# The mLSTM's output gate as a fifth seven-product pair

## The chip, the cores and the metric

The kernel runs on one core of one Trainium2 chip. The metric is the device time of one execution in microseconds (us), as the median of several runs. A profile is one execution taken by the hardware profiler. The engines are TensorE (PE in the profile, its weight loads PEld), VectorE (DVE), ScalarE (ACT), GpSimd (POOL) and SyncE (SP, which issues most of the DMA transfers).

## The reference

One layer of an encoder for 256 tokens of width 2048, all in float32: a SwiGLU feed-forward block, a mixer, a second feed-forward block, each followed by a layer norm, and an input embedding at the end. The mixer, which is all that the change touches, projects its input once and runs two branches:

```python
proj = x @ w_in                                   # 2048 -> 11272 columns
mq, mk, mv, mo, mi, mf, sq, sk, sv, ga, gb = _split_cols(proj)
qk = jax.nn.silu(_causal_conv(jnp.concatenate([mq, mk], axis=-1), conv_w))
...
h = _mlstm_chunkwise(q heads, k heads, v heads, log_i, log_f)       # 4 heads of 256
h = _head_norm(h, norm_g)
y_m = h * jax.nn.sigmoid(mo)                                        # mo: 1024 columns, the output gate
y_sb = _stick_breaking(_heads(sq, 8), _heads(sk, 8), _heads(sv, 8)) # 8 heads of 128
merged = jax.nn.sigmoid(ga) * (y_m @ w_up_m) + jax.nn.sigmoid(gb) * (y_sb @ w_up_sb)
return merged @ w_out
```

## The kernel before, in words

**Matmuls.** The activations stand transposed in on-chip memory as two parts, a rounded high part and the remainder; every weight tile is split in the same way. A product takes three matmuls (high x high, high x low, low x high: lines 1213 to 1215). The work is cut in *units*: one weight tile of 256 rows by up to 512 columns, one half (128) of the 256 tokens, six matmuls. An ordinary column group of 512 needs 8 weight tiles x 2 token halves = 16 units, and each weight tile serves two units.

**Seven products.** `seven` (line 321) computes two column groups at once, as a 2 x 2 block product with seven instead of eight block products: 28 units instead of 32. Some of its products need sums of weight tiles: `grow` (line 337) adds a second tile during a DMA that the GpSimd queue issues, `plus` (line 342) adds on VectorE. Each of its units has a weight tile of its own to split. Its intermediate results go through two reserved accumulator banks (`seeded`). The merge gates ga and gb (four pairs, `gates7`) and most of the feed-forward blocks already use it.

**Weights on their way.** A raw tile is loaded by SyncE (line 1135), rounded by ScalarE (line 1162), and VectorE subtracts to get the low part (line 1166). Raw tiles, split tiles and most other data share 44 buffers of one size, called pages. How many raw tiles and split tiles the plan holds at a time is set by `rooms`: in the mixer 8 to 13 raw tiles and, over the woven part, 4 split tiles; the feed-forward blocks use 16 and 5.

**Order.** The kernel is unrolled by a planner in Python. The list `main` holds the ordinary units: the columns of q, k, v, the output gate and the attention branch, then part of the up projection. `chained` makes a list of the four pairs with gaps between their products, and `weave` spreads this side list evenly over `main`. After each unit the planner's clock advances and generators that are due emit their steps, with the waits in `DELAY` (us) between steps: the convolution (`conv`), the mLSTM heads (`mlstm`), the attention heads (`stick`). Every engine carries out its instructions in the order in which the planner emitted them. `wait` holds a generator until flags are set; it is a wait of the planner, not of an engine.

**The output gate.** `main` has 16 units for each of two column groups g; `mo_done` applies the sigmoid straight from the accumulator and lets GpSimd multiply by the head norm's weights (line 790). Heads 2g and 2g+1 are spawned just ahead of these units, begin when their q, k, v and the gates i and f are there, and wait for the output gate late, ahead of line 857, where the normalised head is multiplied by it. In a head, line 817 is the first matmul, line 821 a select on GpSimd, lines 828 and 840 the further matmuls, line 866 the transposes. In `stick`, lines 882 and 895 to 896 are the first matmuls, 891 and 900 selects on GpSimd, and line 906 the last matmuls, which read what line 900 writes; `DELAY["s2"]` stands between them. Line 677 transposes columns of the attention branch for `sb_turn`, and line 683 copies them out. `away` and `back` put the finished mLSTM output into device memory and fetch it again (line 808). `sched.until` steps generators ahead of their due time when a buffer is lacking.

Of the kernel before, what the change touches and what calls it, by code (L numbers as in the profile page):

```python
# [10 lines left out]
ACT = mybir.ActivationFunctionType  # L11
ALU = mybir.AluOpType
# [4 lines left out]
D = 2048  # L17
# [6 lines left out]
COL = 512  # L24
# [19 lines left out]
DELAY = {  # L44
    "gb": 12.0, "form": 14.0, "form1": 30.0, "ln_turn": 3.4, "ln_step": 1.2, "ln_low": 2.6, "h": 8.0, "silu": 6.0, "late": 9.0, "rest": 1.2, "mt": 3.2,
    "sbt": 6.0, "g0": 3.0, "g1": 4.0, "g2": 12.0, "cv0": 1.0, "cv1": 6.0, "turn": 3.5, "apart": 9.0, "copied": 2.5, "away": 6.0, "refill": 14.0, "cv2": 1.3,
    "m0": 3.0, "m1": 0.6, "m2": 1.2, "m3": 4.6, "m4": 4.6, "s0": 6.6, "s1": 6.7, "s2": 4.0,
}


# [106 lines left out]
def weave(main, side):  # L157

    n = sum(isinstance(u, Unit) for u in main)
    out, at, seen = [], 0, 0  # L160
    for u in main:
        out.append(u)
        if isinstance(u, Unit):
            seen += 1
            while at < len(side) and at * n < seen * len(side):
                if side[at] is not None:
                    out.append(side[at])
                at += 1
    return out
# [11 lines left out]
def kernel(  # L181
# [23 lines left out]
    sched = Sched()  # L205
# [13 lines left out]
    def big(shape=(P, 1024)):  # L219
        return page_pool.tile(list(shape), F32, name="big", tag="page")  # L220
# [16 lines left out]
    def activate(out, in_, func, **kw):  # L237
        use_table(func)
        nc.scalar.activation(out, in_, func, **kw)  # L239
# [11 lines left out]
    xres = [res_pool.tile([P, D], F32, name=f"xres{t}") for t in range(TT)]  # L251
# [136 lines left out]
    program = []  # L388

    def rooms(*n):  # L390
        return lambda: room.__setitem__(slice(0, len(n)), n)
# [5 lines left out]
    class Norm:  # L397
# [206 lines left out]
    st = {}  # L604
# [43 lines left out]
    def wait(*names):  # L648
        while not all(f in flags for f in names):
            yield 0.6  # L650
# [84 lines left out]
    def qk_done(which, g):  # L735
        stage = {}

        def done(ps, t):
            stage[t] = temp()
            nc.scalar.copy(stage[t][:], ps)  # L740
            if t == TT - 1:
                sched.spawn(conv(which, g, stage), DELAY["cv0"])
        return done
# [37 lines left out]
        st["nm"] = big()  # L781
        nc.sync.dma_start(out=st["nm"][:], in_=norm_m[0].partition_broadcast(P))

    def mo_done(g):
        def done(ps, t):
            if ("mo", t) not in st:
                st["mo", t] = big()
            cs = slice(g * COL, (g + 1) * COL)
            activate(st["mo", t][:, cs], ps, ACT.Sigmoid)
            nc.gpsimd.tensor_tensor(out=st["mo", t][:, cs], in0=st["mo", t][:, cs],  # L790
                                    in1=st["nm"][:, cs], op=ALU.mult)
            flags.add(("mo", t, g))
# [18 lines left out]
        return tl[:, 0:512].rearrange("q (a s) -> q a s", s=S)[:, :, 0:P]  # L811

    def mlstm(h):
        yield from wait("gates", ("qk", 0, h), ("qk", 1, h), ("v", 0, h // 2), ("v", 1, h // 2))
        d = temp()
        ps = misc([P, S])
        nc.tensor.matmul(ps[:], st["sel"][:, h], st["M"], start=True, stop=True)
# [39 lines left out]
        nc.vector.reciprocal(out=rstd[:], in_=rstd[:])  # L857
        for t in range(TT):
            nc.vector.tensor_scalar(out=hs[:, t], in0=hs[:, t], scalar1=mv[:, t, 0:1], scalar2=rstd[:, t],
# [85 lines left out]
    ga0 = sq0 + 3 * HS * DS  # L945
    gt = {}

    def gates7(g):

        def place(t, half):  # L950
            if (g, t) not in gt:
                assert g > 1 or "spilt" in flags
                gt[g, t] = xres[t][:, g * 1024:(g + 1) * 1024] if g < 2 else big()[:]
            return gt[g, t][:, half * COL:(half + 1) * COL]

        def done(m, banks):
            ps = {k: v["ps"][:] for k, v in banks.items() if v}
            if m == 5:
                e = temp()
                nc.scalar.copy(e[:], ps["E"])  # L960
                banks["B"]["ps"], banks["W"]["ps"] = seeded
                nc.vector.tensor_tensor(out=banks["B"]["ps"][:], in0=ps["X"], in1=e[:], op=ALU.subtract)
                drop()
            elif m == 6:
                nc.scalar.copy(banks["W"]["ps"][:], ps["B"])
            elif m == 4:
                nc.scalar.copy(place(1, 0), ps["E"])
            elif m == 2:
                sched.spawn(gate(0, 0, ps["X"], 1.0), DELAY["silu"])
            elif m == 7:  # L970
                c = place(1, 0)
                nc.vector.tensor_tensor(out=c, in0=ps["W"], in1=c, op=ALU.add)
                sched.spawn(gate(1, 0, c, 1.0), DELAY["silu"])
            elif m == 3:
                sched.spawn(gate(0, 1, ps["B"], -1.0))
                sched.spawn(gate(1, 1, ps["W"], -1.0))
# [7 lines left out]
        return seven(w_in[:, ga0:ga0 + D], w_in[:, ga0 + D:ga0 + 2 * D], D, g * COL, COL, x1T, done)  # L984

    def up_done(g, half):
        def done(ps, t):
# [19 lines left out]
    main.insert(len(main) - 4, back)  # L1007
# [245 lines left out]
```

## Time and profile before

| | |
|---|---|
| median of 3 runs | 2197.73 us (2196.45 to 2198.91) |
| the profiled execution | 2197.17 us, of which the span from first to last instruction is 2195.5 us |
| TensorE busy | 2175.7 us (99%) |
| VectorE busy | 1789.3 us (82%) |
| ScalarE busy | 1333.5 us (61%) |
| GpSimd busy | 241.2 us (11%) |

Busy times say how long an engine had something in work. TensorE's matmuls overlap one another, so its speed is read from the spacing of its matmuls. In groups of instructions, "x8 | 10.0, 1245 | 29.2" is the count, the busy time in us, the mean of one in ns, and the engine's idle time before them, with what ended it. In lists of waits a row names who waited, on what, and the total in us, the number of times and the longest. "L1166" is line 1166 of the kernel.

### The profile page before, as it was taken

Reading aid. Unit: us, or ns where it says so; the run is one execution under the profiler, and the core shown is the slowest. Engines: PE = TensorE matmul, PEld = TensorE weight load, DVE = VectorE, ACT = ScalarE, POOL = GpSimd, SP = SyncE. Lnnn points to the kernel's source line nnn. Section 1 sums busy time; section 2 is a strip of 40 time slices with the busy share of each in tenths; the row PEclk is TensorE's granted clock in tenths of the full one; section 3 lists DMA queues with packets and bytes.
Section 4 is the critical chain, followed back from the end, with each engine's and each line's share of the span. In section 5 each row is a group of like instructions: output and inputs, shape, how many; then the busy total and the mean of one; then the engine's idle time right before and its main releaser. Section 6 shows DMA issues by size and latency. Waiting matters only on the chain.

```text
span 2195.5 us, 27768 instructions
## 1 busy us (share of the span) xinstructions
PE 2175.7 (99%) x9972; PEld 1801.3 (82%) x9972; DVE 1789.3 (82%) x1967; ACT 1333.5 (61%) x1600; POOL 241.2 (11%) x209
## 2 busy tenths in 40 slices
PE   9999999999999999999999999999999999999999
PEld 7888888888887888888887888888888888888878
DVE  6889988888898778877676777599898989889884
ACT  6556565666575666766575644556666666666562
POOL 3111101111100001011022100011011101110000
PEclk9999999999999999999999999999999999999999
DMA  9899889887993858879678876679878998899652
GB/s 347 221 256 268 254 240 301 270 245 208 292 328 115 255 140 255 225 225 270 206 196 252 261 265 200 213 161 316 262 228 243 305 259 248 241 278 300 214 167 72
DMA packets 274346, 527.06 MB, mean 240 GB/s; under 512 B 16640, under 2 KB 25760, under 8 KB 273952
## 3 DMA queue, kind: packets, MB, share of 16 engines
q1 hardware_dynamic: 229248, 435.10, 58.5%
q0 software_dynamic: 44960, 90.19, 22.4%
q8 instruction: 78, 1.28, 0.2%
q14 instruction: 60, 0.49, 0.1%
HBM read 518.93 MB, written 6.29 MB: 239 GB/s over the span
## 4 chain that ended last, share of the span: by engine, by line
PE 94%; DVE 2%; ACT 2%; issue 1%; DMA 1%; POOL 0%; DVEq 0%; ACTq 0%
PE mm L1214 26%; PE mm L1215 25%; PE mm L1213 25%; PE seeded L1214 5%; PE seeded L1215 5%; PE seeded L1213 5%; PE ms L267 1%; DVE split L1166 1%; ACT split L1162 1%; DMA aside<-actT 1%; ACT temp L239 0%; PE ms L456 0%; POOL temp L891 0%; PE ms L906 0%; PE ms L840 0%
## 5 line engine op out<-in xcount | busy, mean ns | idle before, releaser
L1166 DVE TENSOR_TENSOR split<-raw,split 128x1024 fp32r<-128x1024 f32 (+2 forms) x1061 | 1241.6, 1205 | 221.5 <-ACT split L1162 209.5
L1162 ACT CAST split<-raw 128x1024 fp32r<-128x1024 f32 (+2 forms) x1061 | 1066.8, 1038 | 443.0 <-PE mm L1214 119.1
L1213 PE MATMUL mm<-split,actT 128*128 128x512 f32 (+2 forms) x2640 | 1026.7, 389 | 2.8 <-ACT big L1069 2.3
L1214 PE MATMUL mm<-split,actT 128*128 128x512 f32 (+2 forms) x2640 | 1015.3, 385 | 4.7 <-DVE split L1166 4.7
L1215 PE MATMUL mm<-split,actT 128*128 128x512 f32 (+2 forms) x2640 | 1015.3, 385 | 2.3 <-DVE actT L272 2.3
L1214 PEld LDWEIGHTS mm<-split,actT 128*128 128x128 f32 x2640 | 496.4, 188 | 103.0 <-DVE split L1166 8.3
L1215 PEld LDWEIGHTS mm<-split,actT 128*128 128x128 f32 x2640 | 495.9, 188 | 102.1 <-DVE actT L272 3.1
L1213 PEld LDWEIGHTS mm<-split,actT 128*128 128x128 f32 x2640 | 496.2, 188 | 99.7 <-ACT big L1069 3.2
L337 POOL DMA_DIRECT2D raw<-in_ffn_w_dram x128 | 153.9, 1216 | 1159.8 <-DVE split L1166 961.9
L342 DVE TENSOR_TENSOR raw<-raw 128x1024 f32<-128x1024 f32 x160 | 195.3, 1221 | 12.8 <-DMA raw<-in_ffn_w_dram 10.6
L1214 PE MATMUL seeded<-split,actT 128*128 128x512 f32 x480 | 187.1, 390 | 1.8 <-DVE split L1166 1.8
L1213 PE MATMUL seeded<-split,actT 128*128 128x512 f32 x480 | 188.6, 393 | 0.0
L1215 PE MATMUL seeded<-split,actT 128*128 128x512 f32 x480 | 187.0, 390 | 0.0
L571 DVE SCALAR_TENSOR_TENSOR xres<-mm,xres 128x512 f32<-128x512 f32 x160 | 109.1, 686 | 21.9 <-PE mm L1215 21.9
L1214 PEld LDWEIGHTS seeded<-split,actT 128*128 128x128 f32 x480 | 90.2, 188 | 20.6 <-DVE split L1166 2.5
L1215 PEld LDWEIGHTS seeded<-split,actT 128*128 128x128 f32 x480 | 90.1, 188 | 18.8
L1213 PEld LDWEIGHTS seeded<-split,actT 128*128 128x128 f32 x480 | 90.2, 188 | 18.0
L269 ACT CAST actT<-ms 128x512 fp32r<-128x512 f32 x60 | 35.2, 587 | 85.2 <-PE ms L267 85.1
L337 POOL DMA_DIRECT2D raw<-in_w_in_dram x32 | 38.5, 1208 | 269.8 <-DVE split L1166 262.8
L272 DVE TENSOR_TENSOR actT<-ms,actT 128x512 fp32r<-128x512 f32 x60 | 41.1, 686 | 25.0 <-ACT actT L269 15.2
L239 ACT ACTIVATE temp<-mm 128x512 f32<-128x512 f32 (+1 forms) x38 | 21.8, 574 | 57.8 <-PE mm L1215 57.8
L235 ACT ACT_TABLE_LOAD x36 | 46.2, 1283 | 0.6
(154 smaller groups left out, 724.5 us busy)
## 6 DMA issues: line engine op xcount, KB each, us to landing
raw<-in_ffn_w_dram SPq DMA_DIRECT2D x527, 512.0 KB, 8.0
raw<-in_w_in_dram SPq DMA_DIRECT2D x168, 512.0 KB, 5.0
raw<-in_ffn_w_dram POOLq DMA_DIRECT2D x128, 512.0 KB, 9.4
raw<-in_w_in_dram POOLq DMA_DIRECT2D x32, 512.0 KB, 8.1
raw<-in_w_out_dram SPq DMA_DIRECT2D x32, 512.0 KB, 4.9
raw<-in_w_ple_gate_dram SPq DMA_DIRECT2D x24, 512.0 KB, 5.4
raw<-in_w_up_m_dram SPq DMA_DIRECT2D x16, 512.0 KB, 5.3
raw<-in_w_up_sb_dram SPq DMA_DIRECT2D x16, 512.0 KB, 5.2
```

Of the source, the lines that this page charges most:

```text
L235: nc.scalar.preload_act_table_set(table[0])
L267: nc.tensor.transpose(ps[:, k], src[:, k * P:(k + 1) * P], ident[:])
L269: nc.scalar.copy(dst[:, 0], ps[:])
L272: nc.vector.tensor_tensor(out=dst[:, 1], in0=ps[:], in1=dst[:, 0], op=ALU.subtract)
L337: nc.gpsimd.dma_start(out=raw.tile[:, :, :cols], in_=src.src, accum_op=ALU.add)
L342: nc.vector.tensor_tensor(out=a.tile[:, :, :cols], in0=a.tile[:, :, :cols], in1=b.tile[:, :, :cols], op=ALU.add)
L571: nc.vector.scalar_tensor_tensor(out=xs, in0=ps, scalar=0.5, in1=xs, op0=ALU.mult, op1=ALU.add)
L1162: nc.scalar.copy(hi[:, ks], r[:, ks])
L1166: nc.vector.tensor_tensor(out=lo[:, ks], in0=r[:, ks], in1=hi[:, ks], op=ALU.subtract)
L1213: nc.tensor.matmul(ps, hi, w[0][:, k, :u.cols], start=first, stop=False, skip_group_check=u.onto)
L1214: nc.tensor.matmul(ps, hi, w[1][:, k, :u.cols], start=False, stop=False, skip_group_check=u.onto)
L1215: nc.tensor.matmul(ps, lo, w[0][:, k, :u.cols], start=False, stop=last, skip_group_check=u.onto)
```

## The change

The output gate's 1024 columns leave `main` and become a fifth seven-product pair, first in the side list: its two column groups are the two halves of the pair. The code of `gates7` that finishes the products becomes `sigmoid7`, with the place of the result and what follows the sigmoid handed in; for the output gate that is the multiplication on GpSimd. With `main` shorter (200 units instead of 232) and the side list longer (163 places instead of 132), `weave` puts side units closer together. Heads wait for both token halves of their output gate ahead of their first step instead of ahead of line 857. One delay (`s2`) and two rooms are changed. The edit of the line with `back` leaves its place as it was.

```diff
-    ... "s0": 6.6, "s1": 6.7, "s2": 4.0,
+    ... "s0": 6.6, "s1": 6.7, "s2": 5.5,
...
-    def mo_done(g):
-        def done(ps, t):
-            if ("mo", t) not in st:
-                st["mo", t] = big()
-            cs = slice(g * COL, (g + 1) * COL)
-            activate(st["mo", t][:, cs], ps, ACT.Sigmoid)
-            nc.gpsimd.tensor_tensor(out=st["mo", t][:, cs], in0=st["mo", t][:, cs],
-                                    in1=st["nm"][:, cs], op=ALU.mult)
-            flags.add(("mo", t, g))
-        return done
+    def mo_place(t, g):
+        if ("mo", t) not in st:
+            st["mo", t] = big()
+        return st["mo", t][:, g * COL:(g + 1) * COL]
+
+    def mo_after(t, g):
+        c = mo_place(t, g)
+        nc.gpsimd.tensor_tensor(out=c, in0=c, in1=st["nm"][:, g * COL:(g + 1) * COL], op=ALU.mult)
+        flags.add(("mo", t, g))
...
     def mlstm(h):
-        yield from wait("gates", ("qk", 0, h), ("qk", 1, h), ("v", 0, h // 2), ("v", 1, h // 2))
+        yield from wait("gates", ("qk", 0, h), ("qk", 1, h), ("v", 0, h // 2), ("v", 1, h // 2),
+                        ("mo", 0, h // 2), ("mo", 1, h // 2))
...
         yield DELAY["m3"]
-        yield from wait(("mo", 0, h // 2), ("mo", 1, h // 2))
...
         if g:
-            main += [rooms(9)] + columns(COL, COL, qk_done(0, 1)) + [rooms(9)] + columns(1024 + COL, COL, qk_done(1, 1))
+            main += [rooms(9)] + columns(COL, COL, qk_done(0, 1)) + [rooms(8)] + columns(1024 + COL, COL, qk_done(1, 1))
...
         main.append(lambda g=g: sched.spawn(in_sequence([mlstm(2 * g), mlstm(2 * g + 1)])))
-        main += columns(3072 + g * COL, COL, mo_done(g))
...
         if first in (2, 20):
-            main.append(rooms(12 if first == 2 else 10))
+            main.append(rooms(12 if first == 2 else 7))
...
-    def gates7(g):
+    def sigmoid7(wa, wb, col0, place, after):
         def done(m, banks):
...
             elif m == 2:
-                sched.spawn(gate(0, 0, ps["X"], 1.0), DELAY["silu"])
+                sched.spawn(part(0, 0, ps["X"], 1.0), DELAY["silu"])
...
-        def gate(t, half, src, sign):
+        def part(t, half, src, sign):
             activate(place(t, half), src, ACT.Sigmoid, scale=sign)
-            flags.add(("gate", g, half, t))
+            after(t, half)
...
-    program.extend(weave(main, chained([gates7(g) for g in range(4)])))
+    program.extend(weave(main, chained([sigmoid7(w_in[:, 3072:], w_in[:, 3072 + COL:], 0, mo_place, mo_after)] + [gates7(g) for g in range(4)])))
```

More of the change, by code (lines that the diff above doesn't have):

```diff
@@ L46 @@
     "sbt": 6.0, "g0": 3.0, "g1": 4.0, "g2": 12.0, "cv0": 1.0, "cv1": 6.0, "turn": 3.5, "apart": 9.0, "copied": 2.5, "away": 6.0, "refill": 14.0, "cv2": 1.3,
-    "m0": 3.0, "m1": 0.6, "m2": 1.2, "m3": 4.6, "m4": 4.6, "s0": 6.6, "s1": 6.7, "s2": 4.0,
+    "m0": 3.0, "m1": 0.6, "m2": 1.2, "m3": 4.6, "m4": 4.6, "s0": 6.6, "s1": 6.7, "s2": 5.5,
 }
@@ L946 @@
     gt = {}
-    def gates7(g):
[L950 to L954, printed above, removed]
+    def sigmoid7(wa, wb, col0, place, after):
         def done(m, banks):
@@ L972, in done, with gates7, place @@
                 nc.vector.tensor_tensor(out=c, in0=ps["W"], in1=c, op=ALU.add)
-                sched.spawn(gate(1, 0, c, 1.0), DELAY["silu"])
+                sched.spawn(part(1, 0, c, 1.0), DELAY["silu"])
             elif m == 3:
-                sched.spawn(gate(0, 1, ps["B"], -1.0))
-                sched.spawn(gate(1, 1, ps["W"], -1.0))
-        def gate(t, half, src, sign):
+                sched.spawn(part(0, 1, ps["B"], -1.0))
+                sched.spawn(part(1, 1, ps["W"], -1.0))
+        def part(t, half, src, sign):
             activate(place(t, half), src, ACT.Sigmoid, scale=sign)
-            flags.add(("gate", g, half, t))
+            after(t, half)
             return
             yield
-        return seven(w_in[:, ga0:ga0 + D], w_in[:, ga0 + D:ga0 + 2 * D], D, g * COL, COL, x1T, done)
+        return seven(wa, wb, D, col0, COL, x1T, done)
+    def gates7(g):
+        def place(t, half):
+            if (g, t) not in gt:
+                assert g > 1 or "spilt" in flags
+                gt[g, t] = xres[t][:, g * 1024:(g + 1) * 1024] if g < 2 else big()[:]
+            return gt[g, t][:, half * COL:(half + 1) * COL]
+        return sigmoid7(w_in[:, ga0:ga0 + D], w_in[:, ga0 + D:ga0 + 2 * D], g * COL, place,
+                        lambda t, half: flags.add(("gate", g, half, t)))
     def up_done(g, half):
@@ L1005, in ups @@
         return flat(group(w_up_m, range(0, HM * DM, 2 * P), g * COL, COL, ymT, up_done(g, 0)))
-    main.insert(len(main) - 4, back)
+    main[len(main) - 4:len(main) - 4] = [back]
     for g in range(3):
         main += ups(g, 0) + [rooms(12)]
-    program.extend(weave(main, chained([gates7(g) for g in range(4)])))
+    program.extend(weave(main, chained([sigmoid7(w_in[:, 3072:], w_in[:, 3072 + COL:], 0, mo_place, mo_after)] + [gates7(g) for g in range(4)])))
     program.append(rooms(10, 6))
```

## The prediction

> **What bounds the kernel now.** I read the page first (busy shares, the slices, the chain that ended last), then the busy times of two long stretches, then who made TensorE wait in the stretch that the change touches.
>
> ```profile
> span 2195.5 us, 27768 instructions
> PE 2175.7 (99%) x9972; PEld 1801.3 (82%) x9972; DVE 1789.3 (82%) x1967; ACT 1333.5 (61%) x1600; POOL 241.2 (11%) x209
> PEclk9999999999999999999999999999999999999999
> PE 94%; DVE 2%; ACT 2%; issue 1%; DMA 1%; POOL 0%; DVEq 0%; ACTq 0%
> ```
>
> TensorE is busy 99% of the span at the full granted clock, and 94% of the chain that ended last is TensorE. A busy TensorE need not be at its peak, so I look at the spacing of its matmuls. Below is the order of time on TensorE in a stretch with nothing but weight matmuls; the first and the last of 25 rows, one matmul each.
>
> ```profile
> 717.04 0.39 PE L1213 MATMUL mm<-split,actT 128*128 128x512 f32 x1
> ...
> 722.48 0.39 PE L1213 MATMUL mm<-split,actT 128*128 128x512 f32 x1
> ```
>
> 24 steps take 5.44 us, 0.227 us each. Now the busy times of the woven part of the mixer (738 to 1242 us, the only stretch whose instructions change), of the first feed-forward block, and of the two parts of the first.
>
> ```profile
> core 0: us, PE busy (x) PEld busy (x) DVE busy (x) ACT busy (x) POOL busy (x), PEclk, DMA share, GB/s
> 738.00:1242.00 504.00, 498.81 (x2303) 410.72 (x2302) 376.42 (x464) 325.83 (x424) 71.62 (x64) 1.00 0.81 230
> 170.00:640.00 470.00, 469.54 (x2101) 388.27 (x2100) 417.16 (x409) 289.34 (x308) 57.32 (x48) 1.00 0.91 263
> 738.00:1105.00 367.00, 365.39 (x1653) 299.63 (x1652) 278.42 (x350) 238.26 (x297) 42.27 (x40) 1.00 0.81 226
> 1105.00:1242.00 137.00, 133.42 (x652) 111.09 (x651) 97.99 (x115) 87.57 (x128) 29.34 (x25) 1.00 0.81 242
> ```
>
> The mixer's stretch loses 504.00 - 498.81 = 5.19 us of TensorE, 3.58 us of it in the last 137 us, where the stick-breaking heads run. The feed-forward stretch loses 0.46 us in 470 although VectorE is busier there (417.16 / 470 = 89% against 376.42 / 504 = 75%) and the DMA engines are too. So load alone costs TensorE nothing; bursts do. Who made TensorE wait, in the mixer's stretch and then (last row) in the feed-forward stretch; columns: total us, times, longest.
>
> ```profile
> PE seeded L1214 <- DVE split L1166: 1.8, 2, 1.2
> PE ms L677 <- DVE big L683: 1.4, 1, 1.4
> PE ms L906 <- POOL temp L900: 0.9, 1, 0.9
> PE mm L1214 <- DVE split L1166: 0.8, 2, 0.7
> PE ms L840 <- DVE temp L830: 0.2, 1, 0.2
> ...
> PE mm L1214 <- DVE split L1166: 0.5, 1, 0.5
> ```
>
> **The change, part by part.** *Matmuls.* The output gate takes 2 column groups x 8 weight tiles x 2 row halves = 32 units of 6 matmuls; as a seven-product pair, 7 products x 4 = 28. That removes 24 matmuls, exactly the 24 steps above: -5.44 us, all on the path. The Trainium skill (TensorE: Matmul & The Clock Gate, "Back-to-back issue gap") gives N/2.4 + 2.5 ns, 216 ns for 512 columns, by which the saving would be 5.2 us and the sum below 0.3 us higher; the measured 0.227 decides.
>
> *What the pair adds off the path.* Rows of the mixer's stretch:
>
> ```profile
> L1166 DVE TENSOR_TENSOR split<-raw,split 128x1024 fp32r<-128x1024 f32 (+1 forms) x226 | 265.2, 1206 | 93.3 <-ACT split L1162 92.3 <-PE mm L1214 0.2
> L342 DVE TENSOR_TENSOR raw<-raw 128x1024 f32<-128x1024 f32 x32 | 39.2, 1224 | 2.2 <-DMA raw<-in_w_in_dram 2.2
> L962 DVE TENSOR_TENSOR seeded<-mm,temp 128x512 f32<-128x512 f32 x4 | 2.8, 697 | 2.1 <-ACT temp L960 2.1
> L1162 ACT CAST split<-raw 128x1024 fp32r<-128x1024 f32 (+1 forms) x227 | 225.1, 1034 | 45.7 <-PE mm L1214 13.5 <-DMA aside<-actT 8.4 <-PE seeded L1214 6.4
> L960 ACT COPY temp<-mm 128x512 f32<-128x512 f32 x4 | 2.3, 585 | 3.4 <-PE mm L1215 3.4
> L337 POOL DMA_DIRECT2D raw<-in_w_in_dram x32 | 38.5, 1208 | 269.8 <-DVE split L1166 262.8 <-DVE hrs L857 7.0
> q0 software_dynamic: 9856, 20.97, 22.6%
> raw<-in_w_in_dram SPq DMA_DIRECT2D x149, 512.0 KB, 5.0
> raw<-in_w_in_dram POOLq DMA_DIRECT2D x32, 512.0 KB, 8.1
> ```
>
> Splits go from 16 to 28. VectorE: 12 x 1.206 + 8 sums (L342) x 1.224 + 2 combinations x 0.697 = 25.7 us, so 402 of some 499 us, 81%. ScalarE: 12 x 1.034 + 3 copies x 0.585 = 14.2 us (four sigmoids stay), 340 us. POOL: 8 accumulating loads x 1.208 = 9.7 us (four products with the norm's row stay). DMA: plain weight loads stay 16; the 8 accumulating ones cost 22.6% of 504 us over 40 transfers of 0.52 MB = 2.85 us each, 23 us, so 0.86 of the engines. All four stay under what the feed-forward stretch carries at a loss of 0.46 us, except ScalarE, which has a third of the stretch free; that headroom is the cover, and I price these loads at nothing on average.
>
> *The bursts.* Four split tiles are kept ready in the mixer. Side units split one tile each, main units one for two: before 116 + 112 tiles over 344 units, after 100 + 140 over 340. Four tiles cover 4 / 0.663 = 6.0 units before, 5.7 after; at 1.36 us a unit 0.5 us less. The four waits for a split (1.8 + 0.8 us) each can grow by that: +2.0 us at most, and 0 by the feed-forward row, where the mix is denser still (332 tiles over 440 units, though with five kept). I take the middle, +1.0.
>
> *The heads.* In the chain in order of time, heads 0 and 1 take their first step here:
>
> ```profile
> 799.02 0.62 PE ms L817 x2
> ...
> 841.08 0.62 PE ms L817 x2
> ```
>
> A head lasts 42 us. Units 0 to 344 of the section fill 504 us, 1.465 us a unit with the small matmuls. Counting the woven order, the pair's seventh product ends at unit 82, its sigmoid follows 6 us later: head 0 starts at some 864 us instead of 799, head 1 ends at 948, and heads 2 and 3, spawned at unit 132 (931 us), overlap head 1 for 17 us. The wait is the planner's own and blocks no engine: behind it stand only the head's later steps and the aside transfers, which come back two hundred us later. The overlap puts two chains on the engines; the one wait of this chain on TensorE was 0.2 us (L840). Between 0 and 1 us; I take +0.4, nearest that row.
>
> *Delay s2, 4.0 to 5.5.* L906 is issued 1.5 us later, past the select (L900) that held it 0.9 us: between 0 and -0.9; I take -0.9, because 1.5 exceeds the wait. *Rooms 9 to 8 and 10 to 7.* Fewer raw tiles are planned ahead, yet the DMA queue's own waits show that pages gate it already:
>
> ```profile
> SPq L1135 <- PE mm L1215: 199.4, 72, 7.2
> SPq L1135 <- DVE split L1166: 89.0, 40, 13.5
> SPq L1135 <- PE seeded L1215: 59.6, 21, 6.1
> SPq L1135 <- PE mm L1214: 39.5, 17, 6.4
> ```
>
> SP stands 388 of 504 us in these four rows, so a smaller room frees the page for the next load earlier rather than delaying it: 0. If that cover is gone, three tiles of 2.74 us (504 us over 184 loads) are lost, 8 us of lead, against 5.0 us to land.
>
> Sum: -5.44 + 1.0 + 0.4 - 0.9 = -4.9 us. The profiled execution took 2197.17 us (span 2195.5 and 1.7 around it), so 2192.2; the median of the runs shown is 2197.73, 0.56 above it and inside their spread.
>
> **Rivals.** *A, as summed: 2192.2,* own range 2190 to 2194.5.
>
> *B, the bursts get better.* The heads leave the first conv steps alone and the sticks are issued with a longer last delay. If the stick stretch's 3.58 us vanish with the four split waits unchanged: 2197.17 - 5.44 - 3.6 = 2188.1. Against it: the splits behind a stick's ScalarE steps still come in bursts.
>
> *C, POOL is locked out more often.* Two groups of POOL selects with their means, the same two with ns shortest/median/longest, and, in order of time, one select beside VectorE's work:
>
> ```profile
> L891 POOL TENSOR_SCALAR_AFFINE_SELECT temp<-temp 128x256 f32<-128x256 f32 x8 | 12.5, 1561 | 54.7 <-DVE temp L890 50.3 <-PE ms L896 4.3
> L900 POOL TENSOR_SCALAR_AFFINE_SELECT temp<-temp 128x256 f32<-128x256 f32 x8 | 10.0, 1245 | 29.2 <-ACT temp L239 29.2
> ...
> L891 POOL TENSOR_SCALAR_AFFINE_SELECT temp<-temp x8: 404/1263/5867, 1098.5 to 1220.8; 128x256 f32<-128x256 f32 x8
> L900 POOL TENSOR_SCALAR_AFFINE_SELECT temp<-temp x8: 402/732/3760, 1111.9 to 1233.4; 128x256 f32<-128x256 f32 x8
> 1185.80 5.87 POOL L891 TENSOR_SCALAR_AFFINE_SELECT temp<-temp 128x256 f32<-128x256 f32 x1 [3.57 <-DVE temp L890]
> 1186.78 4.63 DVE L1166 TENSOR_TENSOR split<-raw,split 128x1024 fp32r<-128x1024 f32 x4
> ```
>
> The same select takes 0.40 us or 5.87 us; the long one ends at 1191.67, just after VectorE's run of splits at 1191.41, and the next select, which TensorE waited for, stood behind it. The Trainium skill (SBUF — State Buffer, "SBUF: two separate sides") says that VectorE and GpSimd take a shared port pair as an exclusive lock, a VectorE operation with two SBUF inputs blocking a GpSimd one that reads SBUF; this row agrees, and the rule speaks against the change. The 16 selects took (8 x 1.561 + 8 x 1.245) about 22.4 us by their durations, 16 over the uncontested 0.40 each. VectorE's idle share falls from 25% to 19%, so this may grow by a third, 5 us. If all of it lands on TensorE and s2 saves nothing: -5.44 + 5 + 1.0 + 0.4 = +1.0, 2198; with half of it 2195.6. Against it: of those 16 us only 0.9 reached TensorE. I put C at 2196.
>
> *D, slower: pages.* Heads 0 and 1 hold four pages (two of q and k, two of v) some 65 us longer. SP is gated by pages, so each page less makes a load 2.74 us later, 11 us in all against the 5.0 us to land and the ready tiles' 7.7 us. If loads then run at the pages' pace, 24 of them in 65 us, each 0.6 us late: +15, 2207. It decides from 0.4 us a load on (10 us). Against it: no ScalarE split waits for a weight load in this stretch; the only wait for one is L342's 2.2 us.
>
> *E, no gain:* TensorE's saving turns into split waits one for one, 2197. The 89% of the feed-forward stretch speaks against it.
>
> **How the numbers follow.** A 0.49, B 0.14, C 0.22, D 0.08, E 0.07. A measurement of this kernel tells about 0.2%, 4.4 us, from no change (its runs span 2.5 us). Faster by more: below 2193.3, most of A (0.42) and B, 0.56. Within: the rest of A, C, E, 0.36. Slower: D, 0.08. The predicted time is A's. The range 2188 to 2198 leaves out D and the tails of B and C; cases of both signs of the bound lie in it, so A's own range stands above.
>
> **What would show it.** Right: 9948 matmuls on the page; 12 more splits and 8 more sums; head 0's first L817 near 864 us; TensorE idle in the woven stretch within 2 us of 5.2; no wait L906 <- L900. Wrong: new TensorE waits for splits beyond 4 us (E), long selects with L906 or L830 behind them (C), or ScalarE splits waiting for raw tiles between 864 and 948 us or in the stretch with room 7 (D).

## The result, and the profile after

The changed kernel takes 2219.35 us in the median (2216.80 to 2220.96) against 2197.28 us (2196.45 to 2198.91) for the kernel before on the same chip: a ratio of 1.0097, interval 1.0083 to 1.0112. It is 22 us slower; forecast were 2192.2 us and 5 us faster. Its profiled execution took 2219.35 us. The page's head and the shares of its chain:

```profile
span 2217.6 us, 27819 instructions
PE 2179.5 (98%) x9948; PEld 1799.4 (81%) x9948; DVE 1813.3 (82%) x1989; ACT 1349.3 (61%) x1617; POOL 255.0 (11%) x217
PE 85%; DVE 6%; ACT 4%; DMA 3%; issue 2%; POOL 0%; DVEq 0%; ACTq 0%; POOLq 0%
```

The work is what was forecast: 24 matmuls fewer (9972 - 9948), VectorE 24.0 us busier, 8 POOL instructions more. But TensorE's share of the chain fell from 94% to 85%. Lines have moved: 1213 to 1215 are now 1216 to 1218, 1162 and 1166 are 1165 and 1169, 891 and 900 are 890 and 899, 866 is 865, 808 is 807. TensorE's waits from 738 to 1260 us, where it had five rows and 5.1 us before:

```profile
PE mm L1216 <- DMA actT<-aside: 6.8, 1, 6.8
PE mm L1217 <- DVE split L1169: 4.9, 7, 1.7
PE ms L840 <- DVE temp L830: 3.7, 3, 2.4
PE ms L817 <- DVE actT L262: 2.8, 2, 1.8
PE seeded L1217 <- DVE split L1169: 1.6, 2, 1.2
PE ms L752 <- ACT temp L740: 1.4, 1, 1.4
PE seeded L1216 <- ACT split L1165: 1.1, 1, 1.1
PE ms L881 <- DVE actT L262: 0.5, 1, 0.5
PE mm L1216 <- ACT split L1165: 0.4, 1, 0.4
PE ms L865 <- DVE temp L860: 0.2, 1, 0.2
PE ms L894 <- POOL temp L890: 0.2, 1, 0.2
```

They add up to 23.6 us, of three kinds: the aside transfer, split operands, and small matmuls of heads and convolution (L840, L817, L752, L881, L865). The windows below (columns as in the prediction: TensorE, its loads, VectorE, ScalarE, GpSimd, granted clock, DMA share, GB/s) are of the kernel before, then of the changed one:

```profile
850.00:1010.00 160.00, 158.55 (x711) 130.00 (x710) 123.41 (x156) 104.20 (x127) 18.34 (x17) 1.00 0.85 241
1190.00:1275.00 85.00, 82.64 (x380) 67.83 (x380) 64.74 (x76) 49.08 (x65) 9.14 (x7) 1.00 0.76 252
```

```profile
850.00:1010.00 160.00, 148.93 (x653) 118.64 (x652) 121.19 (x174) 107.48 (x138) 22.27 (x21) 0.98 0.75 211
1190.00:1275.00 85.00, 76.54 (x333) 61.16 (x333) 60.51 (x67) 48.27 (x66) 9.30 (x5) 0.96 0.86 285
```

From 850 to 1010 us TensorE gets 58 matmuls fewer done, with VectorE no busier (121.19 for 123.41 us). Its busy time hides part of the loss, because stretched matmuls count as busy. I therefore use one more number, *loss*: over all matmuls of a stretch, the time from one start to the next beyond the usual spacing of its shape (0.227 us for 512 columns), worked out from the order of time. It holds waits and half-clock stretches alike. Another choice of the usual spacing moves single entries by up to 1.5 us. The table is in us:

| | 736–850 | 850–1010 | 1010–1190 | 1190–1275 | sum |
|---|---|---|---|---|---|
| before | 2.0 | 4.1 | 4.1 | 4.0 | 14.2 |
| after | 3.8 | 19.8 | 5.0 | 12.6 | 41.2 |
| e2_back | 3.8 | 19.0 | 5.0 | 4.7 | 32.5 |
| f1_delays | 2.4 | 17.5 | 6.4 | 1.7 | 28.0 |
| f5_uneven | 1.1 | 12.0 | 17.9 | 7.0 | 38.0 |
| f6_fill | 3.5 | 19.0 | 9.4 | 1.9 | 33.8 |
| e11_dense | 5.0 | 7.3 | 11.3 | 11.7 | 35.3 |

After less before is 27.0 us; less the 5.4 saved by matmuls that is 21.6, against 22.1 between the two profiled spans. So the cost has two places: 8.6 us behind 1190 us, 15.7 us between 850 and 1010.

*The first place.* The order of time at 1200 us, then the fetch that L1216 waited for, in the changed kernel:

```profile
1200.31 0.77 PE L1216 MATMUL mm<-split,actT 128*128 128x512 f32 x1 [6.82 <-DMA actT<-aside]
1200.87 0.63 PE L1217 MATMUL mm<-split,actT 128*128 128x512 f32 x1
1201.30 0.63 PE L1218 MATMUL mm<-split,actT 128*128 128x512 f32 x1
1201.72 0.63 PE L1216 MATMUL mm<-split,actT 128*128 128x512 f32 x1
```

```profile
L807 POOL DMA_DIRECT2D actT<-aside x4: 814/830/851, 1187.1 to 1188.7; - x4
DMA to landing us min/median/max: 13.1/14.2/15.2
```

The same fetch in the kernel before, which no instruction waited for:

```profile
L808 POOL DMA_DIRECT2D actT<-aside x4: 536/558/585, 1180.0 to 1181.7; - x4
DMA to landing us min/median/max: 6.3/8.1/10.3
```

It is issued 7 us later and takes 6 us longer; behind the stop the matmuls stand 0.43 us apart in place of 0.227.

*The second place.* The order of time around head 1's first step, without the weight matmuls:

```profile
905.88 0.38 PE L865 MATMUL ms<-ident,temp 128*128 128x128 f32 x2
906.24 1.22 DVE L342 TENSOR_TENSOR raw<-raw 128x1024 f32<-128x1024 f32 x1
...
906.92 0.37 ACT L261 CAST actT<-ms 128x256 fp32r<-128x256 f32 x1 [0.20 <-PE ms L865]
...
907.38 2.35 DVE L1169 TENSOR_TENSOR split<-raw,split 128x1024 fp32r<-128x1024 f32 x2
...
909.65 0.75 DVE L262 TENSOR_TENSOR actT<-ms,actT 128x256 fp32r<-128x256 f32 x2
910.12 0.94 PE L817 MATMUL ms<-big 4*128 4x256 f32 x2 [1.84 <-DVE actT L262]
```

Head 0's transposes L865 begin at 905.88. ScalarE's half of their copy is soon through, VectorE's half (L262) waits for nothing but its place in the queue, behind a sum of the pair and two splits, until 909.65; and L817, which needs the accumulator, stops TensorE. No transfer is late here, and VectorE is busy for only 76% of the stretch (121.19 of 160 us): a short step stands behind long ones in an in-order queue.

Over the whole stretch from 850 to 1010 us, TensorE's listed waits are 6.7 us at small matmuls of the heads (L840 3.7, L817 2.8, L865 0.2) and 4.3 us for splits (L1217 and L1216); before they were 0.2 and 1.2 us. Another 2.0 us of the loss are ten steps of 512 columns that took 0.43 us each, in two stretches of lower granted clock (0.57 from 859 to 863 us, 0.51 from 910.4 to 913.9 us). The rest is in excesses too small for the list of waits.

### The profile page after: what moved, and what is told of

The parts are those of the page before. It is cut to its first block, busy times and chain, and to the rows that moved or that the text cites. A ratio compares the mean times of both kernels' runs of the same rounds, so it can differ in the third digit from the quotient of the medians.

```text
span 2217.6 us, 27819 instructions
## 1 busy us (share of the span) xinstructions
PE 2179.5 (98%) x9948; PEld 1799.4 (81%) x9948; DVE 1813.3 (82%) x1989; ACT 1349.3 (61%) x1617; POOL 255.0 (11%) x217
## 4 chain that ended last, share of the span: by engine, by line
PE 85%; DVE 6%; ACT 4%; DMA 3%; issue 2%; POOL 0%; DVEq 0%; ACTq 0%; POOLq 0%
PE mm L1217 23%; PE mm L1218 23%; PE mm L1216 23%; PE seeded L1217 5%; PE seeded L1218 5%; PE seeded L1216 5%; DVE split L1169 3%; ACT split L1165 2%; DMA raw<-in_ffn_w_dram 1%; PE ms L267 1%; ACT temp L239 1%; DMA raw<-in_w_in_dram 1%; DVE temp L763 1%; DMA actT<-aside 1%; ACT L235 1%
## 5 line engine op out<-in xcount | busy, mean ns | idle before, releaser
L1169 DVE TENSOR_TENSOR split<-raw,split 128x1024 fp32r<-128x1024 f32 (+2 forms) x1073 | 1258.3, 1207 | 212.5 <-ACT split L1165 196.5
L1165 ACT CAST split<-raw 128x1024 fp32r<-128x1024 f32 (+2 forms) x1073 | 1079.5, 1038 | 454.0 <-PE mm L1217 121.6
L1216 PE MATMUL mm<-split,actT 128*128 128x512 f32 (+2 forms) x2608 | 1016.3, 390 | 10.1 <-DMA actT<-aside 6.8
L1217 PE MATMUL mm<-split,actT 128*128 128x512 f32 (+2 forms) x2608 | 1004.4, 385 | 8.6 <-DVE split L1169 8.6
L1218 PE MATMUL mm<-split,actT 128*128 128x512 f32 (+2 forms) x2608 | 1003.9, 385 | 2.3 <-DVE actT L272 2.3
L1217 PEld LDWEIGHTS mm<-split,actT 128*128 128x128 f32 x2608 | 491.1, 188 | 107.4 <-DVE split L1169 13.9
L1216 PEld LDWEIGHTS mm<-split,actT 128*128 128x128 f32 x2608 | 490.8, 188 | 106.6 <-issue 7.9
L1218 PEld LDWEIGHTS mm<-split,actT 128*128 128x128 f32 x2608 | 490.6, 188 | 100.9 <-DVE actT L272 3.1
L342 DVE TENSOR_TENSOR raw<-raw 128x1024 f32<-128x1024 f32 x168 | 204.8, 1219 | 16.8 <-DMA raw<-in_ffn_w_dram 10.4
L1216 PE MATMUL seeded<-split,actT 128*128 128x512 f32 x504 | 198.3, 393 | 1.1 <-ACT split L1165 1.1
L1217 PE MATMUL seeded<-split,actT 128*128 128x512 f32 x504 | 197.7, 392 | 1.6 <-DVE split L1169 1.6
L1218 PE MATMUL seeded<-split,actT 128*128 128x512 f32 x504 | 196.9, 391 | 0.0
L1217 PEld LDWEIGHTS seeded<-split,actT 128*128 128x128 f32 x504 | 95.0, 189 | 22.7 <-DVE split L1169 3.5
L1216 PEld LDWEIGHTS seeded<-split,actT 128*128 128x128 f32 x504 | 95.0, 189 | 21.0 <-ACT split L1165 1.5
L1218 PEld LDWEIGHTS seeded<-split,actT 128*128 128x128 f32 x504 | 95.1, 189 | 19.7
L337 POOL DMA_DIRECT2D raw<-in_w_in_dram x40 | 48.4, 1218 | 288.7 <-DVE split L1169 244.0
```

The source lines that it names most:

```text
L337: nc.gpsimd.dma_start(out=raw.tile[:, :, :cols], in_=src.src, accum_op=ALU.add)
L342: nc.vector.tensor_tensor(out=a.tile[:, :, :cols], in0=a.tile[:, :, :cols], in1=b.tile[:, :, :cols], op=ALU.add)
L1165: nc.scalar.copy(hi[:, ks], r[:, ks])
L1169: nc.vector.tensor_tensor(out=lo[:, ks], in0=r[:, ks], in1=hi[:, ks], op=ALU.subtract)
L1216: nc.tensor.matmul(ps, hi, w[0][:, k, :u.cols], start=first, stop=False, skip_group_check=u.onto)
L1217: nc.tensor.matmul(ps, hi, w[1][:, k, :u.cols], start=False, stop=False, skip_group_check=u.onto)
```

## The experiments

Times are medians, ratios are to the kernel before, in parentheses their intervals. One interval is some 3 us to either side, so differences below that between two experiments are not told apart.

### Parts of the change alone, on the kernel before

```diff
e3_shift: heads wait for "mo" ahead of their first step; nothing else
e4_tuning: "s2" 4.0 -> 5.5, rooms(9) -> rooms(8), rooms 10 -> 7; nothing else
```

> The kernel before with the early wait alone: the output gate stays in its 32 ordinary units, the heads wait for it ahead of their first step. Heads 0 and 1 then start some 35 us later. Theory H: a part of the loss shows without the pair, 2197 to about 2203. Theory P: no change, 2196 to 2198.

> The kernel before with the three changed constants alone (delay s2 5.5, rooms 8 and 7). The prediction's terms: the 0.9 us wait of line 906 goes and the rooms cost nothing, about 2196.4. Rival: with less room raw tiles come late in the stretch before the up projection and TensorE waits for splits, 2200 or more.

e3_shift: 2198.13 us, 1.0006 (0.9997 to 1.0015). e4_tuning: 2197.01 us, 0.9999 (0.9990 to 1.0009). Neither the early wait nor the delay and rooms cost anything that can be told from nothing; the loss comes with the pair. Two limits: the early wait moves head 0's first step to 829.6 us here, and to 871.0 us in the changed kernel; and the delay and the rooms were changed together, so a gain of one could hide a cost of the other.

### Parts undone, on the changed kernel

```diff
e1_late: the wait for "mo" back ahead of line 856
e2_back: -    main[len(main) - 4:len(main) - 4] = [back]
         +    main[len(main) - 12:len(main) - 12] = [back]
```

> The changed kernel with one thing undone: the heads wait for the output gate late again, ahead of the normalised head's multiplication, so heads 0 and 1 start early as before the change. Theory H (the later heads): their steps fell on the second convolution, on the gate's sigmoids and on heads 2 and 3, and held four pages longer; TensorE's loss from 850 to 1010 us goes from about 20 us back to some 5, and the time from 2219 to about 2205. Theory P (the pair itself: denser side units, more work for VectorE): the loss stays, 2215 to 2220.

> The changed kernel with the return of the mLSTM output from device memory issued 8 main units earlier. Theory R (the return lands late): TensorE's 6.8 us wait for it near 1200 us and about 1.6 us at half clock behind it go, 2219 to about 2211. Rival (pages): the four pages taken earlier make weight loads late instead, and the time stays at 2216 or more.

e1_late: 2223.37 us, 1.0118 (1.0103 to 1.0133); with the late wait it is 4 us slower, above the range of either theory, so later heads are not what costs. e2_back: 2211.40 us, 1.0063 (1.0046 to 1.0080), 8 us less. There the fetch goes out 15 us earlier and no longer stops TensorE:

```profile
L807 POOL DMA_DIRECT2D actT<-aside x4: 533/560/585, 1172.5 to 1174.3; - x4
DMA to landing us min/median/max: 3.6/5.4/6.6
```

The loss behind 1190 us falls from 12.6 to 4.7. Theory R had forecast about 2211 us. The first place is settled; all that follows builds on e2_back or on before.

### Single suspects taken away

```diff
e5_nosum:   plus(...) of the output gate's pair -> None (its 8 sums are left out)
e6_qkfirst: the columns of q and k for heads 2, 3 right behind the first ones
e7_split5:  rooms(13, 4) -> rooms(13, 5)
e9_free2:   two pages freed: the head selector and the norm's weights are left out
e10_notable: Silu (L766), Sqrt (L854), the pair's Sigmoid -> Copy (left out)
e12_all:    e5_nosum + e9_free2 + e10_notable
e8_pages42 (kernel before): PAGES = 44 -> 42
```

> The changed kernel with the earlier return (2211.4) and without the 8 sums of weight tiles on VectorE in the output gate's pair (line 342; its second token half and two products are then left incomplete); loads and pages are the same. Theory V (VectorE's in-order queue: the sums wait for two raw tiles each and hold up the splits, beside the second convolution): the loss from 850 to 1010 us falls from 19 to some 8 us, about 2201. Theory L (raw loads late for lack of pages): the splits wait for the same loads, 2208 or more.

> The changed kernel with the earlier return and another order of the main units: the second group of q and k columns right behind the first, then v and heads 0 and 1, then v and heads 2 and 3. The second convolution's steps then fall on the pair's first products, not on its sums and last products. Theory C (the bursts of the second convolution, the pair's end and the heads' first steps fall together): the loss from 850 to 1010 us falls to some 6 us, about 2198. Theory D (side units too dense for four ready tiles anywhere): it moves elsewhere, 2208 or more.

> The changed kernel with the earlier return and five ready split tiles instead of four in the woven mixer, for one raw tile's worth of pages twice over. Theory D (cover too thin): 1.9 us more cover for each burst, 2211 to about 2200. Theory L (pages): two pages less for raw tiles, loads land later, 2215 or more.

> The changed kernel with the earlier return and two pages more for raw and split tiles: the head selector's page and the norm weights' page are left out (heads read a sum over the four heads there, and the gate is multiplied by itself). Theory L (pages): loads run two tiles, 5 us, further ahead; the waits of VectorE's sums and ScalarE's splits for loads go, and of the 19 us lost from 850 to 1010 us at least 6 go, 2205 or less. Theory T (bursts on the in-order queues): 2209 to 2212.

> The changed kernel with the earlier return; the convolution's silu, the head norm's square root and the output gate's sigmoid become plain copies, so that ScalarE loads no activation table between them (those functions are left out). From 850 to 1010 us ScalarE has 15 table loads of 1.283 us, before the change 9. Theory T (bursts, above all of table loads in front of splits): the loss there falls from 19 to some 10 us, about 2202. Theory L: 2209 or more.

> The changed kernel with the earlier return and three things at once: no table loads between the mixer's small functions, two pages more, no sums of weight tiles in the output gate's pair (all these parts of the computation are left out). If these three carry the loss it nearly ends, 2192 to 2196; what stays over 2197 is neither of them but the plain number of splits per time.

> The kernel before with 42 pages instead of 44. Theory L, the prediction's rival D (pages): each page less makes a load 2.7 us later, the smallest margins of the mixer are used up, and its stretch loses 5 us or more there, 2203 and up. If the lead is ample: 2197 to 2199.

| | us | ratio | against e2_back |
|---|---|---|---|
| e5_nosum | 2208.03 | 1.0049 (1.0033 to 1.0066) | -3.4 |
| e6_qkfirst | 2210.59 | 1.0060 (1.0045 to 1.0075) | -0.8 |
| e7_split5 | 2215.86 | 1.0086 (1.0071 to 1.0101) | +4.5 |
| e9_free2 | 2209.99 | 1.0058 (1.0043 to 1.0073) | -1.4 |
| e10_notable | 2207.91 | 1.0046 (1.0029 to 1.0063) | -3.5 |
| e12_all | 2205.20 | 1.0035 (1.0022 to 1.0048) | -6.2 |
| e8_pages42 | 2209.07 | 1.0059 (1.0044 to 1.0074) | before +11.9 |

e5, e9, e10 and e12 leave out parts of the computation and only serve to price them. None of these is the cause by itself: where a theory had named one of the first five or e12_all as the carrier of the loss, the time stayed 5 to 16 us above its forecast. The sums and the table loads between ScalarE's functions may give 3.5 us each; even all three together leave 8 us over before, with 5.4 us of matmuls already saved. A fifth split tile, for which raw tiles have two pages less, is 4.5 us worse, in the range of theory L. Two pages more hardly help the changed kernel. Two pages fewer cost the kernel before 11.9 us, but the expectation had put at least 5 of these into the mixer, and by the loss only some 3 us lie there (736 to 1275 us). Some 5 us lie in the first feed-forward block, where 2080 matmuls are done in place of 2101, and some 4 behind 1500 us:

```profile
170.00:640.00 470.00, 466.91 (x2080) 385.29 (x2080) 412.53 (x405) 285.39 (x302) 57.36 (x48) 1.00 0.89 259
```

So e8_pages42 says little about pages in the mixer.

### The density of side units, without the pair

```diff
e11_dense (kernel before): chained([gates7(g) for g in range(4)]) + [None] * 57
```

> The kernel before, its four pairs woven as densely as after the change (0.815 places a main unit; the side list then ends early and the last main units run alone); the output gate stays ordinary. Theory D (the density of side units alone): the loss from 850 to 1010 us rises from 4 to 12 us or more, 2205 and up. Theory T or L with the later heads: 2197 to 2201.

2219.91 us, 1.0104 (1.0089 to 1.0119). No instruction is added: blank places only make `weave` set the same side units at 0.815 for each main unit in place of 0.57, as in the changed kernel. It loses 21 us more than before. 7.7 us of these lie behind 1190 us, where this kernel's side list has run out and attention heads stand on bare main units, which the changed kernel does not have; 13.4 us are left. They do not lie where the expectation put them: from 850 to 1010 us the loss is 7.3 us, and 12 or more were forecast; 7.2 us more than before are lost from 1010 to 1190 us, where the last steps of heads 2 and 3 now fall. Its two heaviest waits from 1010 to 1275 us:

```profile
PE ms L906 <- POOL temp L900: 4.9, 2, 3.2
PE ms L866 <- DVE actT L262: 4.5, 1, 4.5
```

The first belongs to the attention heads behind 1190 us. The second is the wait at a head's transposes for L262, VectorE's half of their copy, as in the changed kernel. Behind this stop at 1024 us the granted clock is 0.50 from 1028 to 1038 us, and 14 steps of 0.43 us cost another 2.8 us; so one event makes more than half of the 13.4 us. Density alone makes the second place's kind of loss, in this one interleaving; the 13 us are no price per unit.

### Longer delays, a page, a wider weave

```diff
f1_delays (on e2_back): "cv0" 1.0 -> 3.0, "m1" 0.6 -> 3.0, "m4" 4.6 -> 6.6
         -            yield DELAY["m2"]      # between heads, in in_sequence
         +            yield 4.0
f2_page (on f1_delays), f4_before_page (on before):
         -        nc.tensor.matmul(ps[:], st["sel"][:, h], st["M"], ...)
         +        nc.tensor.matmul(ps[:], ident[0:HM, h:h + 1].broadcast_to([HM, P]), st["M"], ...)
f3_wide (on f2_page): ups(g, 1), g < 3, moved into main; rooms(12) -> rooms(9)
```

> The changed kernel with the aside brought back earlier (2211.4 us), and on top of it longer delays between steps of the mixer: 3.0 us in place of 0.6 between the step with L830 and the one with L840, 3.0 in place of 1.0 ahead of L752, 6.6 in place of 4.6 ahead of a head's last step, 4.0 in place of 1.2 between one head and the next. No work is added or removed. Theory S: with more side work per main unit the queues of VectorE and ScalarE lag by 1 to 3 us, and the steps come out sooner than their operands: the stops at L840, L817, L865 and L752 with the half clock behind them make about 9 us of what the stretch 850 to 1010 us loses; with the delays they go, and the time is 2201 to 2204 us. Rival T: the loss is that of the splits, which come late for the woven matmuls whatever the heads do; the stops at the heads then move to L1216 and L1217, and the time stays at 2208 to 2213 us.

> The kernel with the longer delays, and one page of SBUF more in the pool for split operands and raw tiles: the selector that spreads a head's row over the partitions is read from the identity by a broadcast instead of from a tile of its own. Nothing is left out. If raw tiles that land late in 850 to 1010 us are a cause beside the delays, one page gives 1 to 3 us more than the delays alone (two pages gave 1.4 us without the delays); if not, the two agree within 1 us.

> The kernel before with one page of SBUF more, by the selector read from the identity, and nothing else changed. One page less cost 11.9 us. If the kernel before is short of pages everywhere, one more gives 2 to 6 us (2191 to 2195 us); if 43 pages are just enough for it, the time is the same within 1 us.

> The kernel with the longer delays and the page, and the up projections of three more column groups moved from behind the woven stretch into its main list (room 9 in place of 12 behind the first ones), so that the pair's matmuls stand among 224 main units and not among fewer: 163 side to 224 main, 0.73. If the loss goes with the density of the side units, it falls by another 3 to 6 us, to 2197 to 2200 us; if the pages are the limit, the raw tiles of the up projections land later still and the time is 2205 us or more.

f1_delays: 2206.67 us, 1.0047 (1.0032 to 1.0063), 4.7 us less and between the two theories. The stops at L840, L817 and L752 are gone, but from 850 to 1010 us the loss only falls from 19.0 to 17.5. Its waits there, and where the largest comes from:

```profile
PE ms L865 <- DVE temp L763: 4.7, 1, 4.7
PE mm L1217 <- DVE split L1169: 4.7, 5, 1.2
PE seeded L1217 <- DVE split L1169: 0.6, 1, 0.6
```

```profile
910.08 0.38 PE L865 MATMUL ms<-ident,temp 128*128 128x128 f32 x2
...
911.42 1.51 DVE L763 SCALAR_TENSOR_TENSOR temp<-ms,cw,temp 128x253 f32<-128x253 f32 x3
...
913.47 1.51 DVE L763 SCALAR_TENSOR_TENSOR temp<-ms,cw,temp 128x253 f32<-128x253 f32 x3 [0.54 <-ACT temp L239]
...
915.13 0.41 PE L865 MATMUL ms<-ident,temp 128*128 128x128 f32 x2 [4.66 <-DVE temp L763]
```

With the delays moved, a head's transposes stand behind the convolution's two groups of three on VectorE. The stops have changed place: rival T is right that most of the loss stays, theory S about the 4.7 us that were gained, most of them outside this stretch. f2_page: 2206.29 us, 1.0044 (1.0030 to 1.0057), and f4_before_page: 2197.02 us, 1.0000 (0.9992 to 1.0009): a page more is worth nothing in either kernel. (The expectation of f4_before_page speaks of one page less; e8_pages42 took two.) f3_wide: 2216.05 us, 1.0087 (1.0073 to 1.0101), 9.8 us worse than f2_page, with 18.0 us lost from 1100 to 1190 us. By its expectation that is the branch "the pages are the limit". TensorE's two longest waits there are 1.8 us each, one for a split behind ScalarE and one for a GpSimd select that took 7.01 us; no run here separates pages from the other things that the move shifts.

### Density or neighbours

```diff
f5_uneven (on f1_delays): weave's share of side units 0.65 over the first 88 main units, 0.95 behind them
f6_fill (on f1_delays): columns of sq0 + 2 * DS moved to behind the spawn of heads 0 and 1
```

> The kernel with the earlier return of the aside and the longer delays (2206.7 us), its seven-product units now spread unevenly: 0.65 for each main unit over the first 88 main units, the stretch of the convolutions and heads, and 0.95 over the other 112; until now 163 to 200, 0.815, all along (before: 130 to 232, 0.56). Theory D, density: the loss in 850 to 1010 us (17.5 us here, 4.1 before) is of side work that crowds the heads and convolutions; it falls by 6 us or more, the stretches behind give back 1 to 3, and the time is 2200 to 2204 us. Rival N, neighbours: the loss is of the order of the main list, where the second convolution now runs beside heads 0 and 1 because the 32 units of the old gate columns no longer stand between; then spreading the side work moves it by less than 2 us, and the denser second half makes the time 2207 us or more.

> The kernel with the earlier return of the aside and the longer delays (2206.7 us); its first sixteen stick-breaking units (columns of four heads, from behind the second heads) now stand where the old gate columns of heads 0 and 1 stood, between these heads and the second q and k columns. Work and density are the same. Rival N, neighbours: with light main units beside heads 0 and 1 as before, the loss in 850 to 1010 us falls by 6 us or more, to 2198 to 2202 us. Theory D, density: the side work crowds whatever stands there, the loss moves by less than 2 us, and the time is 2205 to 2209 us.

f5_uneven: 2215.79 us, 1.0083 (1.0066 to 1.0100). f6_fill: 2212.51 us, 1.0073 (1.0058 to 1.0088). Light units beside the heads (f6_fill) do not help: the loss from 850 to 1010 us is 19.0, no less than f1_delays' 17.5, with the same 4.7 us stop at L865, so rival N falls. The time is above theory D's range too. (The expectation of f5_uneven counts 130 places for before; the list has 132.) The density shows on both sides of the step in f5_uneven: thinner, 17.5 becomes 12.0; denser, from 1010 to 1190 us, 6.4 becomes 17.9. Theory D had asked for a fall of 6 and a better time; the fall was 5.5, the time got worse by the denser part, and 12.0 is still three times what the kernel before loses there at 0.57. In the dense part the wait is another one, for a raw tile. VectorE's order of time in f5_uneven, whose edit moves the lines of the changed kernel by one (L343 is the sum, L1170 the split):

```profile
1169.05 0.69 DVE L1170 TENSOR_TENSOR split<-raw,split 128x512 fp32r<-128x512 f32 x1 [1.45 <-ACT split L1166]
1174.34 1.23 DVE L343 TENSOR_TENSOR raw<-raw 128x1024 f32<-128x1024 f32 x1 [4.60 <-DMA raw<-in_w_in_dram]
1175.48 1.22 DVE L1170 TENSOR_TENSOR split<-raw,split 128x1024 fp32r<-128x1024 f32 x1
```

At 0.95 the second operand of a sum has not landed, and TensorE stops 4.9 us for the split behind it.

**What is settled and what is not.** Shown: 8 us of the loss are the late fetch of the aside; placing side units as densely as the changed kernel does costs some 13 us even where no work is added (e11_dense), more than half of it in one stop and the slow steps behind it; thinning them takes 5.5 us off the stretch from 850 to 1010 us (f5_uneven); no single suspect of VectorE, ScalarE or the pages accounts for it. Not settled: why the stretch from 850 to 1010 us keeps 12.0 us of loss when it is thinned to 0.65, and 17.5 us when its delays are lengthened. That long VectorE instructions ahead of short steps hold TensorE is shown at single places (909.65 us in the changed kernel, 911.42 in f1_delays), not for the sum. The pair in another place of the chain was not tried. No version beat the kernel before; the best that computes everything is f2_page at 2206.29 us.

## Why the prediction was wrong, step by step

- *Matmuls, -5.44:* right. 9948 on the page, and it is the saving with which the balance of loss comes out (21.6 for 22.1 us).
- *Added work:* right in amount for VectorE, +24.0 us (25.7 forecast), and ScalarE, +15.8 (14.2); GpSimd +13.8 (9.7) is more. One reading was wrong: the prediction says that all but ScalarE stay under what the feed-forward stretch carries, but GpSimd's 81 of 499 us are 16%, against 57.32 of 470 us there, 12%. TensorE's only wait for it was 0.2 us, so nothing came of that.
- *That work priced at nothing, and bursts at +1.0 (0 to +2.0):* the step that failed. I took the cover from the feed-forward stretch, 89% VectorE at a loss of 0.46 us, and counted how many units four split tiles cover, 6.0 to 5.7. But that stretch has no convolutions and heads: none of its groups of VectorE instructions takes less than 0.68 us in the mean, and TensorE's one wait there is for a split. In the mixer short steps stand behind the long ones and TensorE behind the short ones. Waits for splits grew from 2.6 to 8.0 us, +5.4 where +2.0 was the most allowed. The loss from 850 to 1010 us grew by 15.7 us; that holds this term, the heads' term below and the half clock behind both, and no run parts them. A row from another stretch gave the price of the load, not of the load together with what it meets.
- *Density:* the numbers were there ahead of the prediction (132 places over 232 units, 163 over 200), but I only used them for the count of split tiles. e11_dense loses some 13 us by the density alone.
- *Aside transfers, "come back two hundred us later":* true in time and wrong as a reason. The place of `back` is counted in main units from the end, and I did not price the queue there; the stop was 6.8 us and the loss 8.6 more than before.
- *Heads' overlap, +0.4 (0 to 1):* mis-sized. L840 and L817 alone wait 6.5 us in place of 0.2, while the waits for splits in the same stretch grew from 1.2 to 4.3. The 0.2 was the price of the heads' chain beside the sparser side units of the kernel before; whether the overlap or the denser side units raised it stays open. The start was near: first L817 at 871.0 us, 864 forecast; and in e3_shift the early wait by itself is free.
- *s2, -0.9:* the wait for L900's successor is gone as forecast, but with the rooms the edit moved the time by no more than 0.2 us (e4_tuning). *Rooms, 0:* no cost that this run shows; it holds both.
- *Rival C (GpSimd locked out):* the trace again shows one select between 0.41 and 6.95 us, but TensorE's only wait for one is 0.2 us (L894). It fell.

```profile
L890 POOL TENSOR_SCALAR_AFFINE_SELECT temp<-temp x8: 407/1270/6953, 1089.8 to 1231.0; 128x256 f32<-128x256 f32 x8
```

- *Rival D (pages, raw tiles late):* had the sign and nearly half of the way in time (2207 us), by another mechanism. L342 waits 6.4 us for raw tiles in place of 2.2, but its mark hardly came: no split of ScalarE waits for a raw tile between 864 and 948 us, the one long wait (2.4 us at 1194 us) falls into TensorE's stop for the aside, and pages given back are worth no more than 1.4 us (e9_free2, f2_page).
- *Rival E (the saving turns into split waits):* its mark, new split waits above 4 us, came: 8.0 - 2.6 = 5.4. Its price of 5.4 was only the first part of the bill.

## What to carry to other kernels

An engine's load is priced in the stretch where it lands, with the short steps that stand in the same in-order queue: name the longest instruction that can stand ahead of each short step on which TensorE waits, and ask how often the new work puts it there. When an interleaving becomes denser, test the density alone, with blanks in place of work; it costs one run and here it showed some 13 us that no count of work had. And whatever is placed by counting units from an end has to be looked up again when the list changes.

## What the runs showed of the hardware

A stop costs more than its length. Behind the 6.8 us stop at 1200 us the matmuls stood 0.43 us apart for seven steps at a granted clock of 0.50 (1200 to 1204 us); with the slower steps at either end that is some 1.8 us more; the granted clock of the window from 1190 to 1275 us is 0.96 in the row above. The same followed at 910 us in the changed kernel, behind a stop of 2.2 us (the matmul before L817 began at 907.88), and at 860 us, behind steps of 1.5 and 1.75 us in a row (granted clock 0.57 from 859 to 863 us), while the 2.8 us stop at 957 us had one slow step behind it and no lower clock (1.00 from 956 to 961 us). The Trainium skill (TensorE: Matmul & The Clock Gate, "What's actually happening") says that the clock is halved after an idle window of about 3.4 us that runs freely; the stop of 6.8 us agrees, those at 860 and 910 us are shorter than the window it names.

```profile
907.88 0.40 PE L1218 MATMUL mm<-split,actT 128*128 128x512 f32 x1
910.12 0.94 PE L817 MATMUL ms<-big 4*128 4x256 f32 x2 [1.84 <-DVE actT L262]
910.99 0.80 PE L1216 MATMUL mm<-split,actT 128*128 128x512 f32 x1
911.58 0.63 PE L1217 MATMUL mm<-split,actT 128*128 128x512 f32 x1
912.01 0.63 PE L1218 MATMUL mm<-split,actT 128*128 128x512 f32 x1
912.44 0.63 PE L1216 MATMUL mm<-split,actT 128*128 128x512 f32 x1
```
